# Turning two heads, two key tiles and two output tiles per block of transposes, and moving the context states beside the first level products

## The chip, the cores and the metric

The kernel runs as one program on one core of a Trainium2 chip. The metric is device time in microseconds, the median of several runs. TensorE (PE) multiplies and transposes and writes to PSUM, eight banks of 128 x 512 words in float32; ScalarE (ACT) and VectorE (DVE) read PSUM and work in SBUF; SyncE (SP) and GpSimd (POOL) issue most transfers. Each engine takes its instructions from a queue in a fixed order and waits for semaphores of the others.

## The reference

One block of a network with two branches on 256 tokens of width 2048, with 256 context tokens beside them:

```python
xn = rmsnorm(h, norm_gain) * (1 + scale) + shift        # cn for the context likewise
aq, ak, av, ag, hq, hff, hfb, hi, hg, ma, mb = split_columns(xn @ w_in)
# branch 1: window attention, 16 heads in 4 groups, keys of tokens and of context, one sink logit per head
att_branch = window_attention(q, k, v, k_c, v_c, sink) * silu(ag)
# branch 2: a gated linear recurrence in both directions; the context gives its start states
s_f = hgrn2_final_state(ck_f, cv_h, cg_f)               # s_b from the flipped context
o = hgrn2_bidir(q_h, v_h, k_f, g_f, k_b, g_b, s_f, s_b)
hg_branch = rmsnorm_per_head(o) * silu(hg)
y = sigmoid(ma + b0) * (hg_branch @ w_o_hgrn) + sigmoid(mb + b1) * (att_branch @ w_o_attn)
out = rmsnorm(h + gate * (y @ w_out)) * final_gain
```

## The kernel before

Nearly all time goes into products with weights in float32. Each weight chunk (128 x 1024 values) is loaded, rounded by ACT into `wh` (line 76), and DVE takes the rest `wl = raw - wh` (line 77); a product is then three float32r matmuls of 512 columns, high by high, low by high, high by low (`mm3`, lines 82 to 85). Three buffers each of `wh` and `wl` and four of `raw` go round. One chunk feeds 12 to 24 matmuls. Results `pj` rotate through four PSUM banks. The other four banks have one buffer each and are called `tp`, `o`, `al1` and `al2`.

Between these projections stands work in plain float32: transposes (a matmul against the identity) and small products. A function that does such work is a generator; each `yield` hands over to a generator of projection chunks, the filler, so that PE has weights to multiply while ACT and DVE prepare the next step. In the recurrence `weave` (line 739) takes as many filler chunks as the yielded number says, in units of 24 matmuls of 512 columns. In the attention `alternate` (line 751) takes a fixed number of chunks per yield.

Inside `tc.manual_schedule(engines={PE})` the order on PE is the order in which the program is written. ACT, DVE, SP and POOL are ordered at build time by a planner, which simulates the machine and at each moment gives an engine the ready instruction of highest priority: attention has 2 * PRIO, weight chunks PRIO, the rest none. The resulting order is fixed in each queue. From line 1045 on PE too is left to the planner.

The steps around the change:

- `pair` (line 476), eight times, two heads of the recurrence each. Lines 623 to 625 turn the outputs of the pair before (`to`, four transposes into `tp`). Lines 627 to 633 transpose the four decay blocks `E` into `tw` and copy them as `wT` into the second half of the tile `X2`. After a unit of filler, lines 635 to 645 multiply `wT` with the context values into `sb` (16 products of 128 columns, bank `o`), the context states, which ACT copies negated. Then `grow` (VectorE) and `copies` (ScalarE) prepare the level products; `grow(1)` writes its totals `TT` into the second half of `X2`, where `wT` lies. After 1.5 units, 128 products in column strips of 32 (`level`, line 562, bank `a1`) follow.
- `keys` (line 927): four key tiles, four transposes each into `tp`, each followed by a `split`: ACT copies the bank rounded (line 884), DVE subtracts that from the bank (line 885). Two filler chunks after each tile.
- `attend` (line 971): 35 iterations. Iteration n computes the scores of head n (`scores`, three matmuls into `al1` or `al2` by turns, then mask, maximum, exponential, scaling by DVE and ACT into `pr`), one filler chunk, then for every fourth head the product with the values (`values`, 12 matmuls into `o`, evicted by line 1011 and split into `bH`, `bL`), then `turned(n - 2)`: the probabilities of head n - 2 are transposed into `tp` and split into `pT`; then one more filler chunk. A score product starts only when the last readers of its bank are done.
- `part_b` (line 1053): for each of four column blocks the merged output `y` of the two token tiles, by two DVE operations each (lines 1057 and 1058), is transposed into `tp` and split.

Of the kernel before, what the change touches and what calls it, by code (L numbers as in the profile page):

```python
# [7 lines left out]
F32 = mybir.dt.float32  # L8
F32R = mybir.dt.float32r
U8 = mybir.dt.uint8  # L10
AF = mybir.ActivationFunctionType
# [3 lines left out]
P = 128  # L15
# [23 lines left out]
def block_kernel(ctx: ExitStack, tc: tile.TileContext, x, c, cx, c_ctx, w_ada, b_ada, norm_gain, w_in,  # L39
# [14 lines left out]
    ps = ctx.enter_context(pl("ps", 1, space=PSUM))  # L54
# [119 lines left out]
    def alt():  # L174
        turn[0] ^= 1
        return f"al{turn[0] + 1}"
# [299 lines left out]
    def pair(g, p, grp, F, banks_q):  # L476
# [52 lines left out]
        def copies(b):  # L529
            for slots, a in ((kslot, 0), (qslot, 1)):  # L530
                if b in slots:
                    dst, src = slots[b], mix(a, 3 - 2 * a, 0, 512, b)
                    if len(dst.shape) == 3:
                        for h in range(2):
                            act.activation(dst[:, h].rearrange("p (n two b) -> p n two b", two=2, b=b),
                                           mix(a, 3 - 2 * a, h * T, T, b), AF.Copy)
                    else:
                        act.activation(dst.rearrange("p (n two b) -> p n two b", two=2, b=b), src, AF.Copy)  # L538
# [49 lines left out]
        def grow(b):  # L588

            n2 = 512 // (2 * b)  # L590
            if b == 1:
                even = [F[d][:, :, 0:T].rearrange("p h (n two) -> p h n two", two=2)[:, :, :, 0] for d in range(2)]
                odd = [F[d][:, :, 0:T].rearrange("p h (n two) -> p h n two", two=2)[:, :, :, 1] for d in range(2)]
            else:
                tv = tots[b].rearrange("p d (n two) -> p d n two", two=2)
                even, odd = tv[:, :, :, 0], tv[:, :, :, 1]
            toff = 1024 - 2 * 512 // b
            Tn = TT[:, toff: toff + 2 * n2].rearrange("p (d n) -> p d n", d=2)
            if b == 1:
                for d in range(2):  # L600
                    for a, par, f in ((d, 0, odd[d]), (2 + d, 1, even[d])):
                        av = v3(A[:, a, :]).rearrange("p h (n two) -> p h n two", two=2)[:, :, :, par]
                        dve.tensor_tensor(av, av, f, op=ALU.mult)
                    dve.tensor_tensor(v3(Tn[:, d, :]), even[d], odd[d], op=ALU.mult)
            else:
                for a0, par, f in ((0, 0, odd), (2, 1, even)):
                    av = A[:, a0: a0 + 2, :].rearrange("p a (n two b) -> p a n two b", two=2, b=b)[:, :, :, par, :]
                    dve.tensor_tensor(av, av, f.unsqueeze(3).to_broadcast([P, 2, n2, b]), op=ALU.mult)  # L608
                dve.tensor_tensor(Tn, even, odd, op=ALU.mult)
            tots[2 * b] = Tn  # L610
# [7 lines left out]
            return ps.tile([P, 512], F32, tag=alt(), name="al")  # L618

        copies(1)  # L620
        yield 0.5

        for f in done:
            f()
        done[:] = []
        yield 0.5
        wT = X2[:, 1024:].rearrange("p (a s) -> p a s", a=8)
        for d in range(2):
            tw = ps.tile([P, 512], F32, tag=alt(), name="tw")
            for i in range(2):  # L630
                for s in range(2):
                    pe.transpose(tw[:, (2 * i + s) * P: (2 * i + s + 1) * P], E[:, d, i, s * P: (s + 1) * P], ident)
            act.activation(wT[:, 4 * d: 4 * d + 4, :], tw.rearrange("p (a b) -> p a b", a=4), AF.Copy)
        yield 1.0
        so = hp.tile([P, 2, 512], F32, tag="so", name="so")
        qslot[64] = so[:, 1]
        S = so[:, 0, :].rearrange("p (d h v) -> p d h v", d=2, h=2)
# [1 line left out]
        for d in range(2):  # L639
            for i in range(2):  # L640
                o = sb[:, (2 * d + i) * HD: (2 * d + i + 1) * HD]
                for s in range(2):
                    pe.matmul(o, wT[:, 4 * d + 2 * i + s, :], vc[:, s, (2 * p + i) * HD: (2 * p + i + 1) * HD],  # L643
                              start=s == 0, stop=s == 1)
        act.activation(so[:, 0, :], sb, AF.Copy, scale=-1.0)

        grow(1)
        copies(2)
        grow(2)
        copies(4)  # L650
        yield 1.5
        a1 = al_bank()
        for z, b in enumerate((0, 1, 2, 4)):
            level(a1, z * P, b)
        for b in (4, 8, 16, 32):
            grow(b)
            copies(2 * b)
# [225 lines left out]
    def split(dh, dl, src, **kw):  # L883
        act.activation(dh, src, AF.Copy, **kw)
        dve.tensor_tensor(dl, src, dh.bitcast(F32), op=ALU.subtract)
# [11 lines left out]
    with tc.manual_schedule(engines={mybir.EngineType.PE}):  # L897
# [27 lines left out]
            split(XH[:, rows, :], XL[:, rows, :], bv[t].rearrange("p (r c) -> p r c", r=2))  # L925

        def keys():
            for t in range(4):
                tk = ps.tile([P, 512], F32, tag="tp", name="tkk")
                for j in range(4):  # L930
                    pe.transpose(tk[:, j * P: (j + 1) * P], kr[:, t, j, :], ident)

                dst = [X[:, t // 2: 8: 2, (t % 2) * P: (t % 2 + 1) * P] for X in (XH, XL)]
                split(dst[0], dst[1], tk.rearrange("p (j t) -> p j t", j=4))
                yield

        def group_in(j, st):
# [33 lines left out]
        def attend(sts):  # L971

            prs, pTs = {}, {}

            def scores(n):
                j, t, i = n // 8, n // 4 % 2, n % 4
                h = 4 * j + i
                sc = ps.tile([P, 512], F32, tag=alt(), name="sc")
                mm3(sc.rearrange("p (a k) -> p a k", a=2), [X[:, t, i, :] for X in sts[j]["q"]], k_mov(j), True, True)
                mt = sc[:, (1 - t) * P: (2 - t) * P]  # L980
                tri = cs[:, K_TRI + t * P: K_TRI + (t + 1) * P]
                mx = few.tile([P, 4], F32, tag="mx", name="mx", bufs=4)
                dve.tensor_tensor(mt, mt, tri, op=ALU.add)
                dve.tensor_reduce(mx[:, 0:1], sc, mybir.AxisListType.X, ALU.max)
                dve.tensor_scalar(mx[:, 1:2], mx[:, 0:1], sk[:, h: h + 1], -1.0, op0=ALU.max, op1=ALU.mult)
                pr = base.tile([P, 512], F32, tag="sm", name="pr", bufs=3)
                act.activation(pr, sc, AF.Exp, bias=mx[:, 1:2], accum_out=mx[:, 2:3])
                act.activation(mx[:, 3:4], sk[:, h: h + 1], AF.Exp, bias=mx[:, 1:2])
                dve.tensor_tensor(mx[:, 2:3], mx[:, 2:3], mx[:, 3:4], op=ALU.add)
                dve.reciprocal(mx[:, 2:3], mx[:, 2:3])  # L990
                act.activation(pr, pr, AF.Copy, scale=mx[:, 2:3])
                prs[n] = pr

            def turned(n):
                i = n % 4
                if i == 0:
                    pTs[n // 4] = [at.tile([P, 4, 4, P], F32R, tag=tg, name="pT") for tg in ("A", "X2")]
                pT = pTs[n // 4]
                tk = ps.tile([P, 4, P], F32, tag="tp", name="tkp")
                for q in range(4):  # L1000
                    pe.transpose(tk[:, q, :], prs[n][:, q * P: (q + 1) * P], ident)  # L1001
                split(pT[0][:, :, i, :], pT[1][:, :, i, :], tk)

            def values(m):
                j, t = m // 2, m % 2
                pT = pTs[m]
                ob = ps.tile([P, 512], F32, tag="o", name="oba")
                for kt in range(4):
                    mm3(ob, v_st(kt, j), [X[:, kt].rearrange("p h t -> p (h t)") for X in pT], kt == 0, kt == 3)
                br = base.tile([P, 4, P], F32, tag="bb", name="br", bufs=2)  # L1010
                dve.tensor_tensor(br, ob.rearrange("p (h t) -> p h t", h=4), sts[j]["g"][:, :, t * P: (t + 1) * P],
                                  op=ALU.mult)
                hs = slice(4 * j, 4 * j + 4)
                split(bH[:, hs, t * P: (t + 1) * P], bL[:, hs, t * P: (t + 1) * P], br)

            for n in range(35):
                if n < 32:
                    with tc.high_priority(2 * PRIO):
                        scores(n)
                yield  # L1020
                with tc.high_priority(2 * PRIO):
                    if n % 4 == 2 and n > 2:
                        values(n // 4 - 1)
                    if 2 <= n < 34:
                        turned(n - 2)
                yield

# [10 lines left out]
            yield from gates_b(1)  # L1038

        sts = [{} for _ in range(4)]  # L1040
        alternate(keys(), group_in(0, sts[0]), 2)
        alternate(attend(sts), fill(sts), 1)


# [8 lines left out]
    def part_b(n):  # L1053
        by = proj_tok(w_oa, n * 512, b_st, range(2))
        for t in range(2):
            yt = base.tile([P, 512], F32, tag="sm", name="yt", bufs=3)
            dve.tensor_tensor(yt, by[t], sgb[n][:, t, :], op=ALU.mult)  # L1057
            dve.tensor_tensor(y[n][:, t, :], y[n][:, t, :], yt, op=ALU.add)
            tk = ps.tile([P, 4, P], F32, tag="tp", name="tky")
            for i in range(4):  # L1060
                pe.transpose(tk[:, i, :], y[n][:, t, i * P: (i + 1) * P], ident)
            ks = slice(4 * n, 4 * n + 4)
            split(XH[:, ks, t * P: (t + 1) * P], XL[:, ks, t * P: (t + 1) * P], tk)

    for n in range(4):
        part_b(n)
# [126 lines left out]
```

## Time and profile before

| | us |
|---|---|
| median of 3 runs (lowest, highest) | 1636.56 (1636.43, 1636.96) |
| the profiled execution's own time | 1636.14 |
| its span, first to last instruction | 1634.3 |
| PE busy | 1613.9 (99%) |
| DVE busy | 937.0 (57%) |
| ACT busy | 763.4 (47%) |
| recurrence, 190 to 900 us: PE busy | 710.0 of 710 |
| attention, 1160 to 1412 us: PE busy; DVE; ACT | 251.5; 179.5; 180.4 of 252 |

The granted TensorE clock was 0.997 over the span. Times within the trace count from the first instruction. In a timeline row the first number is the start, the second the duration, and `x4` says that four alike instructions were merged into the row; what stands in brackets is the idle time of the engine before it and what ended it. The end of a matmul is modelled, so the distance from start to start is the better measure on PE.

### The profile page before, as it was taken

What the parts mean: (1) busy time and instruction counts of PE and PEld (TensorE: products, weight loads), DVE (VectorE), ACT (ScalarE), POOL (GpSimd) and SP (SyncE); (2) the same over time, 40 slices, a digit from 0 to 9 for tenths busy, and PEclk for the clock granted to TensorE, in tenths of its full rate; (3) what the DMA queues carried; (4) which work ended last, traced back from release to release, by engine and by line L of the source; (5) the groups of instructions that cost most, each with busy time, mean ns of one, the idle gap of its engine ahead of it and who ended that gap; (6) DMA issues with size and microseconds to landing.
All of it is one profiled execution on the core that took longest, in us unless ns stands there. A gap on an engine that the chain in (4) does not pass through costs nothing.

```text
span 1634.3 us, 24809 instructions
## 1 busy us (share of the span) xinstructions
PE 1613.9 (99%) x9882; PEld 1329.3 (81%) x9882; DVE 937.0 (57%) x1463; ACT 763.4 (47%) x1200; POOL 31.4 (2%) x88
## 2 busy tenths in 40 slices
PE   7999999999999999999999999999999999999998
PEld 4558888888888888888888888888888888788887
DVE  4444467536665466645567455235677676555565
ACT  4333454424553345433566443224576787454443
POOL 2000000000000000000000000000000000000000
PEclk9999999999999999999999999999999999999999
DMA  9993444336343453435335555424544454665554
GB/s 356 383 384 109 142 150 149 110 127 195 104 129 117 156 176 106 131 117 177 118 119 176 186 193 193 129 90 142 179 140 146 133 168 157 231 201 192 184 191 140
DMA packets 191427, 274.89 MB, mean 168 GB/s; under 512 B 9776, under 2 KB 112592, under 8 KB 190544
## 3 DMA queue, kind: packets, MB, share of 16 engines
q1 hardware_dynamic: 189344, 268.95, 50.1%
q0 software_dynamic: 1248, 3.25, 0.7%
q8 instruction: 77, 1.26, 0.3%
q10 hardware_dynamic: 720, 1.11, 0.2%
q14 instruction: 38, 0.31, 0.1%
HBM read 271.17 MB, written 2.11 MB: 167 GB/s over the span
## 4 chain that ended last, share of the span: by engine, by line
PE 95%; DMA 2%; DVE 1%; issue 1%; ACT 0%; SPq 0%; POOLq 0%; POOL 0%; ACTq 0%
PE pj L83 24%; PE pj L85 23%; PE pj L84 23%; PE pj L141 7%; PE pj L146 4%; DMA raw<-in_w_ada_dram 2%; PE pa L306 2%; PE al L562 1%; PE pj L396 1%; PE pj L389 1%; PE sb L643 1%; PE tkp L1001 1%; PE pj L390 1%; PE oba L83 0%; PE sc L85 0%
## 5 line engine op out<-in xcount | busy, mean ns | idle before, releaser
L77 DVE TENSOR_TENSOR wl<-raw,wh 128x1024 fp32r<-128x1024 f32 x392 | 479.6, 1224 | 425.4 <-ACT wh L76 425.0
L76 ACT ACTIVATE wh<-raw 128x1024 fp32r<-128x1024 f32 x392 | 414.7, 1058 | 589.4 <-PE pj L85 428.6
L84 PE MATMUL pj<-wl,xHL 128*128 128x512 f32 (+1 forms) x1024 | 395.6, 386 | 0.4 <-DVE wl L77 0.4
L85 PE MATMUL pj<-wh,xHL 128*128 128x512 f32 (+1 forms) x1024 | 395.4, 386 | 0.0
L83 PE MATMUL pj<-wh,xHL 128*128 128x512 f32 (+1 forms) x1024 | 391.4, 390 | 0.0
L85 PEld LDWEIGHTS pj<-wh,xHL 128*128 128x128 f32 x1024 | 192.4, 188 | 39.0
L84 PEld LDWEIGHTS pj<-wl,xHL 128*128 128x128 f32 x1024 | 192.5, 188 | 38.2 <-DVE wl L77 0.7
L83 PEld LDWEIGHTS pj<-wh,xHL 128*128 128x128 f32 x1024 | 192.2, 188 | 37.8 <-DVE yt L1057 0.4
L141 PE MATMUL pj<-xHL,wh 128*128 128x512 f32 x512 | 181.1, 396 | 0.0
L83 PE MATMUL pj<-xHL,wh 128*128 128x512 f32 x416 | 164.6, 396 | 0.0
L85 PE MATMUL pj<-xHL,wl 128*128 128x512 f32 x416 | 162.1, 390 | 0.0
L84 PE MATMUL pj<-xHL,wh 128*128 128x512 f32 x416 | 162.0, 389 | 0.0
L146 PE MATMUL pj<-xHL,wl 128*128 128x256 f32 x512 | 139.9, 283 | 0.0
L141 PEld LDWEIGHTS pj<-xHL,wh 128*128 128x128 f32 x512 | 95.0, 188 | 19.2
L84 PE MATMUL pj<-wl,bH 128*128 128x512 f32 x256 | 99.9, 390 | 0.0
L85 PE MATMUL pj<-wh,bL 128*128 128x512 f32 x256 | 99.6, 389 | 0.0
L146 PEld LDWEIGHTS pj<-xHL,wl 128*128 128x128 f32 x512 | 96.7, 189 | 2.5
L85 PEld LDWEIGHTS pj<-xHL,wl 128*128 128x128 f32 x416 | 78.1, 188 | 16.7
L83 PEld LDWEIGHTS pj<-xHL,wh 128*128 128x128 f32 x416 | 78.1, 188 | 15.5
L84 PEld LDWEIGHTS pj<-xHL,wh 128*128 128x128 f32 x416 | 78.2, 188 | 15.4
L83 PE MATMUL pj<-wh,bH 128*128 128x512 f32 x256 | 89.8, 390 | 0.1
L608 DVE TENSOR_TENSOR A<-A,X 128x512 f32<-128x512 f32 x96 | 62.0, 687 | 16.7 <-ACT qk L538 6.7
(278 smaller groups left out, 1688.2 us busy)
## 6 DMA issues: line engine op xcount, KB each, us to landing
raw<-in_w_in_dram SPq DMA_DIRECT2D x292, 512.0 KB, 3.5
raw<-in_w_ada_dram SPq DMA_DIRECT2D x128, 256.0 KB, 5.5
raw<-in_w_ada_dram SPq DMA_DIRECT2D x32, 512.0 KB, 3.7
raw<-in_w_o_hgrn_dram SPq DMA_DIRECT2D x32, 512.0 KB, 3.5
raw<-in_w_o_attn_dram SPq DMA_DIRECT2D x32, 512.0 KB, 3.7
raw<-in_w_out_dram SPq DMA_DIRECT2D x32, 512.0 KB, 4.3
raw<-in_w_in_dram SPq DMA_DIRECT2D x24, 256.0 KB, 5.5
X<-in_x_dram SPq DMA_DIRECT2D x2, 1024.0 KB, 6.7
```

Source lines behind the costliest of these rows:

```text
L76: act.activation(h[:, :n], raw[:, :n], AF.Copy)
L77: dve.tensor_tensor(lo[:, :n], raw[:, :n], h[:, :n].bitcast(F32), op=ALU.subtract)
L83: pe.matmul(o, s[0], m[0], start=first, stop=False)
L84: pe.matmul(o, s[0], m[1], start=False, stop=False)
L85: pe.matmul(o, s[1], m[0], start=False, stop=last)
L141: pe.matmul(banks[i].rearrange("p (a t) -> p a t", a=2), h[:, j, cs_], xHL[:, :, kt, :T], start=kt == 0, stop=kt == KT - 1)
L146: pe.matmul(banks[i][:, :T], lo[:, j, cs_], xH[:, kt, :T], start=False, stop=False)
L306: pe.matmul(pa[32 * g: 32 * g + 32, : 2 * w], cT[:, k0 + g, :], rv_[:, :, g % nk, :], start=k0 == 0, stop=k0 == KT - 4, tile_position=(0, ...
L389: pe.matmul(o, hw, xH[:, kt, :], start=kt == 0, stop=False)
L390: pe.matmul(o, lo[:, kt - k, cs_], xH[:, kt, :], start=False, stop=False)
L396: pe.matmul(o, hw, xL[:, kt, :], start=False, stop=kt == KT - 1)
L608: dve.tensor_tensor(av, av, f.unsqueeze(3).to_broadcast([P, 2, n2, b]), op=ALU.mult)
```

## The change

Five edits, all in the order and the placing of the work; the arithmetic is the same.

1. `pair`: the two yields of 0.5 around the turning of the previous outputs become one of 1.0 ahead of it, so that `to` and `tw` are written one behind the other. `wT` now overwrites `E` in the first half of `X2`. `grow(1)`, `copies(2)`, `grow(2)`, `copies(4)` come directly behind that, then one yield of 2.5, then the 16 context products, and directly behind them the level products. The negated copy of the states follows the level products in the program.
2. `keys`: two tiles' transposes in a row, into `tp` and `o`, then both splits; four filler chunks after each pair of tiles.
3. `scores`: the bank is `al1` for even heads and `al2` for odd ones.
4. `turned`: called on even iterations only; it transposes heads n - 2 and n - 1 in a row, the first into `tp`, the second into `al2`, then splits both.
5. `part_b`: both tiles' merges first, then eight transposes into `tp` and `o` inside a region that orders PE's instructions among themselves, then both splits.

```diff
@@ pair
         copies(1)
-        yield 0.5
+        yield 1.0
         for f in done:
             f()
         done[:] = []
-        yield 0.5
-        wT = X2[:, 1024:].rearrange("p (a s) -> p a s", a=8)
+        wT = X2[:, :1024].rearrange("p (a s) -> p a s", a=8)
...
-        yield 1.0
+        grow(1)
+        copies(2)
+        grow(2)
+        copies(4)
+        yield 2.5
...
-        act.activation(so[:, 0, :], sb, AF.Copy, scale=-1.0)
-        grow(1)
-        copies(2)
-        grow(2)
-        copies(4)
-        yield 1.5
         a1 = al_bank()
         for z, b in enumerate((0, 1, 2, 4)):
             level(a1, z * P, b)
+        act.activation(so[:, 0, :], sb, AF.Copy, scale=-1.0)
@@ keys
-            for t in range(4):
-                tk = ps.tile([P, 512], F32, tag="tp", name="tkk")
...
+            for z in range(2):
+                tks = [ps.tile([P, 512], F32, tag=tg, name="tkk") for tg in ("tp", "o")]
+                for t in range(2):
+                    for j in range(4):
+                        pe.transpose(tks[t][:, j * P: (j + 1) * P], kr[:, 2 * z + t, j, :], ident)
...
@@ attend
-                sc = ps.tile([P, 512], F32, tag=alt(), name="sc")
+                sc = ps.tile([P, 512], F32, tag=f"al{n % 2 + 1}", name="sc")
...
-                tk = ps.tile([P, 4, P], F32, tag="tp", name="tkp")
-                for q in range(4):
-                    pe.transpose(tk[:, q, :], prs[n][:, q * P: (q + 1) * P], ident)
-                split(pT[0][:, :, i, :], pT[1][:, :, i, :], tk)
+                tks = [ps.tile([P, 4, P], F32, tag=tg, name="tkp") for tg in ("tp", "al2")]
+                for i in range(2):
+                    for q in range(4):
+                        pe.transpose(tks[i][:, q, :], prs[n + i][:, q * P: (q + 1) * P], ident)
+                for i in range(2):
+                    z = (n + i) % 4
+                    split(pT[0][:, :, z, :], pT[1][:, :, z, :], tks[i])
...
-                    if 2 <= n < 34:
+                    if n % 2 == 0 and 2 <= n < 34:
                         turned(n - 2)
...
-        alternate(keys(), group_in(0, sts[0]), 2)
+        alternate(keys(), group_in(0, sts[0]), 4)
@@ part_b
-            tk = ps.tile([P, 4, P], F32, tag="tp", name="tky")
-            for i in range(4):
-                pe.transpose(tk[:, i, :], y[n][:, t, i * P: (i + 1) * P], ident)
+        tks = [ps.tile([P, 4, P], F32, tag=tg, name="tky") for tg in ("tp", "o")]
+        with tc.manual_schedule(engines={mybir.EngineType.PE}):
+            for t in range(2):
+                for i in range(4):
+                    pe.transpose(tks[t][:, i, :], y[n][:, t, i * P: (i + 1) * P], ident)
+        for t in range(2):
             ks = slice(4 * n, 4 * n + 4)
-            split(XH[:, ks, t * P: (t + 1) * P], XL[:, ks, t * P: (t + 1) * P], tk)
+            split(XH[:, ks, t * P: (t + 1) * P], XL[:, ks, t * P: (t + 1) * P], tks[t])
```

More of the change, by code (lines that the diff above doesn't have):

```diff
@@ L927, in keys @@
         def keys():
-            for t in range(4):
-                tk = ps.tile([P, 512], F32, tag="tp", name="tkk")
[L930 to L934, printed above, removed]
+            for z in range(2):
[4 more added lines that the diff above has]
+                for t in range(2):
+                    dst = [X[:, z: 8: 2, t * P: (t + 1) * P] for X in (XH, XL)]
+                    split(dst[0], dst[1], tks[t].rearrange("p (j t) -> p j t", j=4))
                 yield
@@ L994, in turned @@
             def turned(n):
-                i = n % 4
-                if i == 0:
+                if n % 4 == 0:
                     pTs[n // 4] = [at.tile([P, 4, 4, P], F32R, tag=tg, name="pT") for tg in ("A", "X2")]
                 pT = pTs[n // 4]
-                tk = ps.tile([P, 4, P], F32, tag="tp", name="tkp")
-                for q in range(4):
-                    pe.transpose(tk[:, q, :], prs[n][:, q * P: (q + 1) * P], ident)
-                split(pT[0][:, :, i, :], pT[1][:, :, i, :], tk)
+                tks = [ps.tile([P, 4, P], F32, tag=tg, name="tkp") for tg in ("tp", "al2")]
[5 more added lines that the diff above has]
+                    split(pT[0][:, :, z, :], pT[1][:, :, z, :], tks[i])
             def values(m):
@@ L1058, in part_b @@
             dve.tensor_tensor(y[n][:, t, :], y[n][:, t, :], yt, op=ALU.add)
-            tk = ps.tile([P, 4, P], F32, tag="tp", name="tky")
-            for i in range(4):
-                pe.transpose(tk[:, i, :], y[n][:, t, i * P: (i + 1) * P], ident)
+        tks = [ps.tile([P, 4, P], F32, tag=tg, name="tky") for tg in ("tp", "o")]
[3 more added lines that the diff above has]
+                    pe.transpose(tks[t][:, i, :], y[n][:, t, i * P: (i + 1) * P], ident)
+        for t in range(2):
             ks = slice(4 * n, 4 * n + 4)
-            split(XH[:, ks, t * P: (t + 1) * P], XL[:, ks, t * P: (t + 1) * P], tk)
+            split(XH[:, ks, t * P: (t + 1) * P], XL[:, ks, t * P: (t + 1) * P], tks[t])
     for n in range(4):
```

## The prediction

> **What bounds the kernel now.** I read the profile's page first, then PE's waits, then PE's timeline at the places that the change touches, and last ACT and DVE between a turning and the score product behind it. Busy time and the chain of work:
>
> ```profile
> span 1634.3 us, 24809 instructions
> ...
> PE 1613.9 (99%) x9882; PEld 1329.3 (81%) x9882; DVE 937.0 (57%) x1463; ACT 763.4 (47%) x1200; POOL 31.4 (2%) x88
> ...
> PE 95%; DMA 2%; DVE 1%; issue 1%; ACT 0%; SPq 0%; POOLq 0%; POOL 0%; ACTq 0%
> ```
>
> PE bounds the kernel: every instruction that PE no longer issues or no longer waits for shortens the end, and every wait put into its queue lengthens it. In the attention and the recurrence PE's waits hold only one group:
>
> ```profile
> PE oba L83 <- DVE qTa L950: 0.5, 3, 0.2
> ```
>
> So no transposed bank and no score bank makes PE wait today. The change takes away no wait that stands in its way; it can gain only what PE loses at the seams between float32r products and float32 transposes.
>
> **What a seam costs.** PE's timeline, first around eight transposes in a row (`tw`), then around four (`tkp`):
>
> ```profile
> 193.84 0.39 PE L85 MATMUL pj<-wh,xHL 128*128 128x512 f32 x1
> ...
> 197.24 0.39 PE L85 MATMUL pj<-wh,xHL 128*128 128x512 f32 x1
> 197.47 1.03 PE L632 MATMUL tw<-cs,X 128*128 128x128 f32 x8
> ...
> 198.57 0.39 PE L84 MATMUL pj<-wl,xHL 128*128 128x512 f32 x1
> ...
> 203.81 1.95 PE L643 MATMUL sb<-vc,X 128*128 128x128 f32 x16
> ...
> 213.54 0.39 PE L85 MATMUL pj<-wh,xHL 128*128 128x512 f32 x1
> 213.86 0.46 PE L562 MATMUL al<-qk 128*32 128x32 f32 x32
> ```
>
> ```profile
> 1179.21 0.60 PE L1001 MATMUL tkp<-cs,pr 128*128 128x128 f32 x4
> ...
> 1179.89 0.39 PE L84 MATMUL pj<-wl,xHL 128*128 128x512 f32 x1
> ...
> 1182.42 0.39 PE L83 MATMUL sc<-xHL,qTa 128*128 128x512 f32 x1
> ```
>
> Fifteen undisturbed products lie between 193.84 and 197.24: 3.40 / 15 = 0.227 us each. From the first of four transposes to the second product behind them are 1179.89 - 1179.21 = 0.68, of which one product is 0.23: four transposes cost 0.45. Eight cost 198.57 - 197.47 - 0.23 = 0.87. Two blocks of four cost 0.03 more than one of eight. The products behind a block are slightly slow: 11 between 1179.89 and 1182.42, 0.230 each, make 11 x 0.0033 = 0.036 per block; 23 between 198.57 and 203.81, 0.228 each, make about 0.026. If that tail too is paid once, a merge saves 0.03 + 2 x 0.036 - 0.026 = 0.08. Bounds 0.03 and 0.08; I take 0.05, since the tail's cause isn't in the rows.
>
> **The change part by part.** The number of transposes, products, splits and DMAs is the same.
>
> Merges: `turned` goes from 32 blocks to 16, `keys` from 4 to 2, `part_b` from 8 to at best 4, and `to` joins `tw` in the last pair (in the other pairs the two already follow each other). That is 16 + 2 + 4 + 1 = 23 merges of 0.05: **-1.1 us** (19 of 0.03 to 23 of 0.08: -0.6 to -1.8).
>
> The context states: 16 products leave a place between float32r products and stand ahead of the strips of `level`. The entry into the strips costs 213.86 - 213.54 = 0.32 instead of 0.23, so 0.09 per pair. If that vanished behind `sb`, eight pairs would give -0.7. But strips behind a block of full-width transposes pay it too:
>
> ```profile
> 27.23 1.04 PE L410 MATMUL idle<-cs 128*128 128x128 f32 x8
> 28.20 1.06 PE L306 MATMUL pa<-raw,cT 128*32 128x512 f32 x8
> ```
>
> Eight transposes are 0.87 and the strips start after 0.97, so 0.10 remain. I take **0** (-0.7 to +0.1, eight times 0.01). The Trainium skill ("TensorEngine Tiling (Array Packing)", Key Properties) says that a change of tiling mode drains TensorE; by that rule the seam merely moves from products to states and the gain is 0, while the -0.7 would need a free change; both entries in the rows agree with it.
>
> `grow(1)` now writes beside `wT` instead of over it, so DVE no longer waits there for the states; DVE sets nothing in this stage (PE is busy throughout), so 0. One copy of the states (like other 512-column copies, 0.6 on ACT) moves into the stretch ahead of the second levels. There the last `grow` ends well before `kt` reads it:
>
> ```profile
> 228.71 1.29 DVE L608 TENSOR_TENSOR A<-A,X 128x512 f32<-128x512 f32 x2
> ...
> 235.80 0.66 PE L669 MATMUL kt<-cs,A 128*128 128x128 f32 x4
> ```
>
> That is 5.8 us of cover; the copy and what it pushes back cost 0, and 0.6 per pair if the cover were gone.
>
> Two heads' probabilities are read earlier: an odd head is turned one iteration sooner. The tightest is head 7, scaled at 1220.10 and turned with head 6 from 1223.39 on:
>
> ```profile
> 1220.10 0.71 ACT L991 ACTIVATE pr<-pr,mx 128x512 f32<-128x512 f32 x1
> ...
> 1223.39 0.60 PE L1001 MATMUL tkp<-cs,pr 128*128 128x128 f32 x4
> ```
>
> 2.6 us remain, so no wait. Each `values` gets its last head two chunks earlier, no wait either.
>
> **The new wait.** The second head goes through `al2`, and the next score product (odd heads) writes `al2`. It must wait until ACT and then DVE have split that bank, and everything behind it on PE waits too. Iteration 12, with the work that lies between:
>
> ```profile
> 1252.61 0.60 PE L1001 MATMUL tkp<-cs,pr 128*128 128x128 f32 x4
> 1252.81 1.06 ACT L76 ACTIVATE wh<-raw 128x1024 fp32r<-128x1024 f32 x1 [2.43 <-PE pj L141]
> ...
> 1253.77 0.58 ACT L884 ACTIVATE pT<-tkp 128x512 fp32r<-128x512 f32 x1
> 1254.08 1.22 DVE L77 TENSOR_TENSOR wl<-raw,wh 128x1024 fp32r<-128x1024 f32 x1
> ...
> 1255.34 0.69 DVE L885 TENSOR_TENSOR pT<-tkp,pT 128x512 fp32r<-128x512 f32 x1
> ...
> 1255.84 0.40 PE L83 MATMUL sc<-xHL,qTa 128*128 128x512 f32 x1
> ```
>
> A chunk ends just ahead of the turning, which frees a weight buffer; so `wh` is ready before the transposed bank and goes first on ACT, and `wl` goes first on DVE. The split ends at 1256.03, after the score product has started; today nobody minds, because `tp` isn't needed for two more chunks. Iteration 14, where `values` evictions share the queues:
>
> ```profile
> 1272.79 0.64 ACT L884 ACTIVATE bH<-br 128x512 fp32r<-128x512 f32 x1
> 1272.83 0.69 DVE L885 TENSOR_TENSOR pT<-tkp,pT 128x512 fp32r<-128x512 f32 x1
> 1273.36 0.40 PE L83 MATMUL sc<-xHL,qTa 128*128 128x512 f32 x1
> 1273.45 0.69 DVE L885 TENSOR_TENSOR bL<-br,bH 128x512 fp32r<-128x512 f32 x1
> ```
>
> The first split in iterations 2, 8 and 10 (iteration 2's next score product is the row of 1182.42 above):
>
> ```profile
> 1182.15 0.69 DVE L885 TENSOR_TENSOR pT<-tkp,pT 128x512 fp32r<-128x512 f32 x1
> ...
> 1226.49 0.69 DVE L885 TENSOR_TENSOR pT<-tkp,pT 128x512 fp32r<-128x512 f32 x1
> 1226.60 0.39 PE L83 MATMUL sc<-xHL,qTa 128*128 128x512 f32 x1
> ...
> 1239.32 0.60 PE L1001 MATMUL tkp<-cs,pr 128*128 128x128 f32 x4
> ...
> 1240.59 0.69 DVE L885 TENSOR_TENSOR pT<-tkp,pT 128x512 fp32r<-128x512 f32 x1
> ...
> 1242.53 0.39 PE L83 MATMUL sc<-xHL,qTa 128*128 128x512 f32 x1
> ```
>
> And what a wait of this kind costs PE beyond its length, from the one that exists:
>
> ```profile
> 1206.38 0.69 DVE L950 SCALAR_TENSOR_TENSOR qTa<-tkq,qTa 128x512 fp32r<-128x512 f32 x1
> 1206.57 0.40 PE L141 MATMUL pj<-xHL,wh 128*128 128x512 f32 x1
> 1207.12 0.50 PE L83 MATMUL oba<-pT,xHL 128*128 128x512 f32 x1 [0.15 <-DVE qTa L950]
> 1207.46 0.40 PE L84 MATMUL oba<-pT,xHL 128*128 128x512 f32 x1
> ```
>
> DVE ends at 1207.07, the product starts 0.05 later, and the next comes 0.34 after it instead of 0.23: 0.16 on top. Back-to-back DVE operations of 512 columns start 1273.45 - 1272.83 = 0.62 apart, so the second split ends 0.62 + 0.69 = 1.31 after the first one starts; the score product would start 0.44 later than now (four more transposes ahead of it). Lateness plus 0.16:
> - iterations like 12 (4, 12, 20): 1255.34 + 1.31 = 1256.65 against 1256.28, so 0.37 + 0.16 = 0.53;
> - like 14 (6, 14, 22): 1274.14 against 1273.80, 0.50 directly behind the first split, 1.12 with `bL` between (0.62 more);
> - like 8 (8, 16, 24): 1227.80 against 1227.04, 0.92;
> - iteration 2: 1183.46 against 1182.86, 0.76;
> - like 10 (10, 18, 26): 1241.90 against 1242.97, no wait; the last ones lie near zero and are left out.
>
> Sum 3 x 0.53 + 3 x 0.92 + 0.76 = 5.1, plus 3 x 0.50 to 3 x 1.12: 6.6 to 8.5, middle 7.5. Against that, odd iterations now have no split, which takes 0.6 each out of ACT's and DVE's queues ahead of the next turning. I give back 0.5 at iterations like 8, where ACT's queue is full, 0.2 at those like 12: 2.1. **+5.4 us.**
>
> The existing wait of `oba` costs 1207.12 - 1206.57 - 0.23 + 0.11 = 0.43, three times 1.3; with a split less ahead of it DVE comes sooner; I take **-0.4** (0 to -1.3).
>
> Sum: 1636.14 (own time of the profiled execution, span 1634.3 and 1.8 around it) - 1.1 - 0.4 + 5.4 = 1640.0. The median is 0.42 above that execution, so **1640.5 us**.
>
> **The rivals.**
> - *The second split is in time.* If ACT takes both banks ahead of `wh`, the second split can end about 2.6 after the first transpose (iteration 10: 1241.90 - 1239.32), and the score product comes after 1182.42 - 1179.21 + 0.44 = 3.65. It decides in favour from the point where the first DVE split starts within 2.3 of the first transpose. For it: priority 2 * PRIO; against it: `wh` is ready first in three of four kinds of turning. Then the merges alone remain, not slower: 1636.56 - 1.1 - 0.4 = 1635.1.
> - *The wait is larger:* nothing is given back and `bL` comes between: 8.5 - 0.6 = 7.9, so 1644.5.
> - *`part_b` doesn't merge.* The region only orders PE's instructions among themselves; the planner may still put a product between the two tiles' transposes. Four merges of 0.05 are lost: 1640.7, inside the forecast.
> - *Merges save more than the rows show,* over 0.2 per seam: 23 x 0.2 - 5.4 is still no gain, so this needs the first rival too: 1632.
>
> **How the numbers follow.** Forecast with a wait of some size, 1637.5 to 1643.5: 0.62; split in time: 0.30; larger wait: 0.05; larger saving: 0.03. A difference under 0.2% (3.3 us) can't be told from none. Of the forecast's case 0.37 of its 0.62 lie above 1639.8, with the larger wait slower is 0.42; of the second case 0.02 falls below 1633.3, so faster is 0.05; same 0.53. The range leaves out half of each outer case: 1634.6 to 1644.0.
>
> **What would show it.** A group of PE's waits "sc L83 <- DVE pT", some 10 times and up to 1 us each; attention longer by 3 to 5 us, the rest within 1; eight-fold `tkp` rows; levels still entered with 0.1 of delay. It is wrong if no score product waits, if odd heads' `tkp` waits for `pr`, or if the recurrence changes by over 1 us.

## The result and the profile after

The changed kernel takes **1651.78 us**, median of 5 runs (1650.43 to 1652.84); the kernel before took 1636.75 beside it (1636.43 to 1637.27). The ratio is 1.0090, with 95% between 1.0079 and 1.0101: slower by 15 us. The profiled execution of the changed kernel is the longest of its five, 1652.84 with a span of 1651.0, 16.7 us above the profiled span of before. The page of the changed kernel, span, busy time and shares of the chain of work:

```profile
span 1651.0 us, 24818 instructions
...
PE 1617.9 (98%) x9882; PEld 1332.6 (81%) x9882; DVE 936.9 (57%) x1463; ACT 765.4 (46%) x1200; POOL 31.4 (2%) x88
...
PE 91%; ACT 4%; DVE 2%; DMA 1%; issue 1%; POOLq 0%; POOL 0%; ACTq 0%; DVEq 0%
```

PE issues the same 9882 matmuls and is still on the chain for nearly all of it, but ACT, which had 0% of the chain, now has 4%: PE waits for it. Busy time of DVE and ACT is what it was, so nobody does more work. The groups of PE's waits in the attention (releaser, total, count, median):

```profile
PE sc L83 <- DVE pT L884: 10.9, 8, 2.1
...
PE oba L83 <- DVE qTa L951: 2.3, 3, 0.8
```

The first group is new; the second was 0.5 for its three. The score products of both kernels (count, durations, start of the first to start of the last), before and then after:

```profile
L83 PE MATMUL sc<-xHL,qTa x32: 389/389/398, 1163.6 to 1391.9; 128*128 128x512 f32 x32
```

```profile
L83 PE MATMUL sc<-xHL,qTa x32: 389/392/501, 1164.7 to 1410.6; 128*128 128x512 f32 x32
```

The stretch from the first to the last score product grew from 228.3 to 245.9, by 17.6. That is all of the loss: the other stages together differ by -0.9 (start +1.15, recurrence +0.2, keys -0.25, `part_b` -0.1, the handover from the attention to the outputs -1.9).

Inside the 17.6, I took PE's distances from start to start and counted what exceeds 0.227. In front of the first score product behind a turning PE stands for these times, by iteration: 2: 0.63; 4, 12, 20: 0.12, 0.20, 0.20; 6, 14, 22: 1.01, 1.01, 1.05; 8, 16, 24: 2.21, 2.26, 2.18; 28: 1.82; the others 0. Sum **12.7**. The product behind each of them comes late as well, 1.2 in all. `oba` takes 1.8 more. Four transposes more lie in the window, 0.4. The last 1.6 stand in one place: behind the wait of iteration 8 the next nine products start 0.33 to 0.43 apart instead of 0.227. The TensorE clock that was granted there was half (stretch, its length, PE's busy time and matmuls, granted clock, DMA share, GB/s):

```profile
1234.20:1236.70 2.50, 2.50 (x7) 0.50 0.36 106
```

No other wait of the attention is followed by such a stretch in this trace. These five make 17.7, which is all of it to within 0.1.

Iteration 8 shows the largest wait (start, duration, engine, line, operation; in brackets the idle time before it and what ended it):

```profile
1227.30 1.03 PE L1003 MATMUL tkp<-cs,pr 128*128 128x128 f32 x8
1227.74 1.04 ACT L76 ACTIVATE wh<-raw 128x1024 fp32r<-128x1024 f32 x1
...
1229.00 0.58 ACT L883 ACTIVATE pT<-tkp 128x512 fp32r<-128x512 f32 x1
1229.60 1.28 ACT L988 ACT_TABLE_LOAD   x1
1230.30 0.68 DVE L884 TENSOR_TENSOR pT<-tkp,pT 128x512 fp32r<-128x512 f32 x1
1230.89 0.69 ACT L988 ACTIVATE pr<-sc,mx 128x512 f32<-128x512 f32 x1
1231.76 0.58 ACT L883 ACTIVATE pT<-tkp 128x512 fp32r<-128x512 f32 x1
1232.37 0.69 DVE L884 TENSOR_TENSOR pT<-tkp,pT 128x512 fp32r<-128x512 f32 x1 [0.33 <-ACT pT L883]
...
1233.11 0.50 PE L83 MATMUL sc<-xHL,qTa 128*128 128x512 f32 x1 [2.05 <-DVE pT L884]
```

Read ACT's rows downward. `wh` goes first, then, behind an activation of a gate that is not shown, the copy of the first bank at 1229.00. The copy of the second bank could follow at 1229.6; but ACT first loads its table (1.28) and takes the exponential of the current head (0.69), and comes to the second bank only at 1231.76. DVE is idle meanwhile but for one small operation and subtracts at 1232.37, and PE, which holds the next score product at the head of its queue, starts it 0.05 after DVE ends.

Iteration 6, where `values` has just been evicted:

```profile
1214.86 0.57 ACT L883 ACTIVATE pT<-tkp 128x512 fp32r<-128x512 f32 x1
1215.43 0.63 ACT L883 ACTIVATE bH<-br 128x512 fp32r<-128x512 f32 x1
...
1215.96 0.58 ACT L883 ACTIVATE pT<-tkp 128x512 fp32r<-128x512 f32 x1
1216.09 0.69 DVE L884 TENSOR_TENSOR bL<-br,bH 128x512 fp32r<-128x512 f32 x1
1216.70 0.68 DVE L884 TENSOR_TENSOR pT<-tkp,pT 128x512 fp32r<-128x512 f32 x1
...
1217.44 0.50 PE L83 MATMUL sc<-xHL,qTa 128*128 128x512 f32 x1 [0.84 <-DVE pT L884]
```

`bH` stands between the two copies, `bL` between the two subtractions. Iterations 12 and 28:

```profile
1260.31 1.03 PE L1003 MATMUL tkp<-cs,pr 128*128 128x128 f32 x8
...
1261.47 1.07 ACT L883 ACTIVATE pT<-tkp 128x512 fp32r<-128x512 f32 x2
...
1262.87 1.28 DVE L884 TENSOR_TENSOR pT<-tkp,pT 128x512 fp32r<-128x512 f32 x2
...
1264.20 0.50 PE L83 MATMUL sc<-xHL,qTa 128*128 128x512 f32 x1
```

```profile
1389.08 1.04 PE L1003 MATMUL tkp<-cs,pr 128*128 128x128 f32 x8
...
1390.36 1.28 ACT L988 ACT_TABLE_LOAD   x1
...
1392.52 1.07 ACT L883 ACTIVATE pT<-tkp 128x512 fp32r<-128x512 f32 x2
...
1394.54 0.50 PE L83 MATMUL sc<-xHL,qTa 128*128 128x512 f32 x1 [1.66 <-DVE pT L884]
```

In iteration 12 both copies follow each other, and so do both subtractions: the wait is 0.20. In iteration 28 both copies follow each other too, but behind a table load and an exponential.

### The profile page after: what moved, and what is told of

Same layout as the page of the kernel before. It is cut to its first block, busy times and chain, and to the rows that moved or that the text cites. A ratio compares the mean times of both kernels' runs of the same rounds, so it can differ in the third digit from the quotient of the medians.

```text
span 1651.0 us, 24818 instructions
## 1 busy us (share of the span) xinstructions
PE 1617.9 (98%) x9882; PEld 1332.6 (81%) x9882; DVE 936.9 (57%) x1463; ACT 765.4 (46%) x1200; POOL 31.4 (2%) x88
## 4 chain that ended last, share of the span: by engine, by line
PE 91%; ACT 4%; DVE 2%; DMA 1%; issue 1%; POOLq 0%; POOL 0%; ACTq 0%; DVEq 0%
PE pj L83 23%; PE pj L85 23%; PE pj L84 23%; PE pj L141 6%; PE pj L146 3%; PE pa L306 2%; PE al L562 1%; PE pj L396 1%; PE pj L389 1%; PE sb L648 1%; PE pj L390 1%; DMA raw<-in_w_ada_dram 1%; ACT wh L76 1%; ACT L969 1%; ACT L988 1%
```

## The experiments

The theory after the result was the predicted one in a larger size: the next score product needs `al2`, and `al2` is free only when the second head is split. The rivals: turning two heads at once loads ACT and DVE in bursts, so that PE waits somewhere whatever bank is used; or the other edits have a share in it.

**One head per turning again.** The attention is put back, the edits of `pair`, `keys` and `part_b` stay.

```diff
-                sc = ps.tile([P, 512], F32, tag=f"al{n % 2 + 1}", name="sc")
+                sc = ps.tile([P, 512], F32, tag=alt(), name="sc")
...
-                tks = [ps.tile([P, 4, P], F32, tag=tg, name="tkp") for tg in ("tp", "al2")]
...
+                tk = ps.tile([P, 4, P], F32, tag="tp", name="tkp")
...
-                    if n % 2 == 0 and 2 <= n < 34:
+                    if 2 <= n < 34:
```

> The changed kernel with only the attention's turning put back: one head per turning into tp, score banks by turns as before; the pair, key and output edits stay. Theory A (the whole loss is PE's waiting in the attention for splits that the turning of two heads makes late: 12.7 us at the score products, 1.3 behind them, 1.8 more at oba): the time returns to 1636.75 less the few merges that are left, 1636.0 to 1636.6. Rival B (the other edits, or the planner's new order that they bring, carry a part of the loss): over 1638.

Measured: 1636.37 against 1636.53, ratio 0.9999 (0.9990 to 1.0009). The three other edits together change nothing that can be measured, and the loss belongs to the attention.

**The second head in another bank.** First `o`, which queries and `values` use:

```diff
-                tks = [ps.tile([P, 4, P], F32, tag=tg, name="tkp") for tg in ("tp", "al2")]
+                tks = [ps.tile([P, 4, P], F32, tag=tg, name="tkp") for tg in ("tp", "o")]
```

> The changed kernel with the second head's transposes in bank o in place of al2. Theory A: the score products no longer wait; the next users of o (the query transposes tkq, twice per group of four iterations pairs, and the value products) wait instead, less often: 1637.5 to 1643. Rival C (two heads in one go overload ACT and DVE in even iterations, so weight chunks or evictions come late whatever the bank is): 1648 or more, with the waits at pj.

Measured: 1651.11, ratio 1.0084 (1.0067 to 1.0101). The time lies where rival C put it, but not for its reason: no `pj` waits. The waits of the score products are gone, and as much stands in another place, which the expectation of theory A had far too small. PE's waits, and one of them in the timeline:

```profile
PE tkp L1003 <- ACT pT L883: 6.5, 3, 2.2
PE tkp L1003 <- DVE br L1015: 4.1, 4, 1.1
```

```profile
1210.51 0.60 PE L1003 MATMUL tkp<-cs,pr 128*128 128x128 f32 x4
...
1213.26 1.08 PE L1003 MATMUL tkp<-cs,pr 128*128 128x128 f32 x4 [2.15 <-ACT pT L883]
```

The wait sits in the middle of the block: four transposes go, and the other four wait until bank `o`, which `values` has just filled, is evicted. For three of the seven waits the profile names the first head's copy, which ends at 1213.15 here; the eviction (DVE, line 1015) ends at 1213.11, and the transposes start 0.15 after that, as they do where the profile names the eviction (1245.34 after 1245.19). So the wait isn't a matter of the bank `al2` as such: it is inherited by whoever needs a bank that is still being read.

Next, one of the four banks through which the projections rotate:

```diff
-                tks = [ps.tile([P, 4, P], F32, tag=tg, name="tkp") for tg in ("tp", "al2")]
+                tks = [ps.tile([P, 4, P], F32, tag="tp", name="tkp"),
+                       pj.tile([P, 4, P], F32, tag="pj", name="tkp")]
```

> The changed kernel with the second head's transposes in one of the four rotating pj banks. Theory A: no score product waits; what is left is the wait of oba for the query split (2.3 us by the trace after): 1637 to 1640, with at most 2 us of new waits of a projection for its bank. Rival C: 1648 or more.

Measured: 1636.61 against 1636.53, ratio 1.0000 (0.9991 to 1.0010), 0.4 below theory A's range. Two heads are still turned in one go and still split one behind the other, and the 15 us are gone. That fells the rival that bursts cost by themselves. Only one group of waits is left in the attention, that of `oba`, and at 2.3 for its three it is as large as in the changed kernel. One of them in the timeline:

```profile
1205.77 0.71 ACT L992 ACTIVATE pr<-pr,mx 128x512 f32<-128x512 f32 x1
1206.38 0.58 ACT L950 ACTIVATE qTa<-tkq 128x512 fp32r<-128x512 f32 x1
1206.99 0.69 DVE L951 SCALAR_TENSOR_TENSOR qTa<-tkq,qTa 128x512 fp32r<-128x512 f32 x1 [0.55 <-ACT qTa L950]
...
1207.73 0.50 PE L83 MATMUL oba<-pT,xHL 128*128 128x512 f32 x1 [0.76 <-DVE qTa L951]
```

In the kernel before, ACT took the queries at once:

```profile
1205.76 0.58 ACT L949 ACTIVATE qTa<-tkq 128x512 fp32r<-128x512 f32 x1
```

An odd head's probabilities are now read one iteration sooner, and the order on ACT has their scaling ahead of the queries' copy; that the planner puts it there for this reason was not tested. `oba` writes the bank `o`, in which the transposed queries `tkq` stand, and so waits 0.76 instead of 0.15.

**The banks exchanged.** The first head goes into `al2`, the second into `tp`.

```diff
-                tks = [ps.tile([P, 4, P], F32, tag=tg, name="tkp") for tg in ("tp", "al2")]
+                tks = [ps.tile([P, 4, P], F32, tag=tg, name="tkp") for tg in ("al2", "tp")]
```

> The changed kernel with the two banks of a turning exchanged: the first head into al2, the second into tp. Work, order of the transposes and of the splits are the same; only the score product now waits for the first split, not for the second. By the first splits' ends in the trace after (1216.15 against a due 1216.43, 1230.98 against 1230.90, 1282.22 against 1282.49) Theory A gives waits of under 2 us in all at the score products: 1638 to 1641. Rival C: 1648 or more.

Measured: 1638.28, ratio 1.0011 (1.0002 to 1.0021). The one wait of a score product that is left, beside the 2.3 of `oba`:

```profile
PE sc L83 <- DVE pT L884: 1.0, 1, 1.0
```

The work, its amount and the four banks are those of the changed kernel, and 13.5 of 15.2 us are gone. The score product waits for the split of the head that stands in its own bank. When that is the first split, it is in time to within 0.15 in all turnings but iteration 28.

**What stands between the two copies.** The second head's rounding goes from ACT to DVE, out of the queue with the table load; `al2` stays.

```diff
-                    split(pT[0][:, :, z, :], pT[1][:, :, z, :], tks[i])
+                    dh, dl = pT[0][:, :, z, :], pT[1][:, :, z, :]
+                    if i:
+                        dve.tensor_copy(dh, tks[i])
+                        dve.tensor_tensor(dl, tks[i], dh.bitcast(F32), op=ALU.subtract)
+                    else:
+                        split(dh, dl, tks[i])
```

> The changed kernel (second head in al2) with the rounding of the second head by DVE in place of ACT: the same number of operations, but no ACT work between the transposed bank and its release. Theory A2 (most of the wait beyond the forecast is ACT's queue: the exponential with its table load, or bH, stands between the two copies): the waits at the score products fall from 10.9 us to under 4: 1638 to 1643. Rival E (DVE's own queue makes the second split late): 1646 or more.

Measured: 1644.81, ratio 1.0049 (1.0035 to 1.0063). That is in neither range: the waits fall from 10.9 to 4.7 + 1.5 = 6.2, not to under 4. PE's waits at the score products, and iteration 8:

```profile
PE sc L83 <- DVE pT L1009: 4.7, 6, 1.4
...
PE sc L83 <- DVE mx L990: 1.5, 3, 0.5
```

```profile
1226.39 1.04 PE L1003 MATMUL tkp<-cs,pr 128*128 128x128 f32 x8
1227.52 0.68 DVE L1008 CAST pT<-tkp 128x512 fp32r<-128x512 f32 x1
...
1229.58 0.68 DVE L1009 TENSOR_TENSOR pT<-tkp,pT 128x512 fp32r<-128x512 f32 x1
1230.41 0.47 PE L83 MATMUL sc<-xHL,qTa 128*128 128x512 f32 x1 [0.25 <-DVE pT L1009]
```

In the iterations like 8 the wait falls from 2.2 to 0.4: there it was indeed ACT's queue, with the table load and the exponential. In iterations 2 and 28 it goes as well, from 0.6 and 1.8 to 0 and 0.1. In those like 14 it rises from 1.0 to 1.5, and in those like 12 from 0.2 to 0.67 (the second group: there the profile names a small DVE operation right behind the second split), since DVE's queue now holds one operation more. So the cause is the order of the queue that the second split goes through; ACT's was the worse one in iterations like 8, in 2 and in 28, DVE's in those like 12 and 14.

**The queries in `tp`.** On top of the version with the `pj` bank, the transposed queries leave bank `o`, so that `oba` no longer waits for them; the same edit is then made alone in the kernel before.

```diff
-                tk = ps.tile([P, 512], F32, tag="o", name="tkq")
+                tk = ps.tile([P, 512], F32, tag="tp", name="tkq")
```

> The kernel with the second head in a pj bank, and the query transposes tkq in bank tp in place of o, so that the value products no longer wait for the query split. Theory A: the three waits of oba (2.3 us, with restart 2.8 against 1.0 before) go, and the merges (16 at 0.02 to 0.055 by the rows, 2 keys, 4 outputs) come out at last: 1633.0 to 1635.0. Rival D (the waits only move to tp, whose first split then holds up tkq or the next turning): 1636 to 1639.

> The kernel before with only the query transposes moved from o to tp. Its three waits of oba cost 0.43 each by the rows. Theory A: 1635.2 to 1635.8. Rival D: 1636.5 or more. The distance to the run with merges then tells what the merges save by themselves: 0.6 to 1.8 by the prediction.

Measured: with two heads per turning 1633.55 against 1636.60, ratio 0.9981 (0.9972 to 0.9989), and no wait of PE is left between 130 and 1600 us; alone in the kernel before 1637.45, ratio 1.0004 (0.9995 to 1.0013). There the wait has moved, to the next turning in `tp`, and grown from 0.5 to 1.7, as rival D has it (waits of that run):

```profile
PE tkp L1001 <- DVE qTa L950: 1.7, 3, 0.6
```

**Is it the merges or the banks?** The version with the queries in `tp` merges 23 times and also has one more bank for turned heads. First the `pair` edit is taken out of it:

```diff
-        yield 1.0
+        yield 0.5
         for f in done:
             f()
         done[:] = []
+        yield 0.5
...
-        grow(1)
-        copies(2)
-        grow(2)
-        copies(4)
-        yield 2.5
+        yield 1.0
...
+        act.activation(so[:, 0, :], sb, AF.Copy, scale=-1.0)
+        grow(1)
+        copies(2)
+        grow(2)
+        copies(4)
+        yield 1.5
```

> The run with second head in pj and queries in tp, with the pair edit undone: context states again one unit and a half ahead of the level products, two yields of 0.5. By the blocks on PE states and levels cost 3.23 us per pair apart (1.80 + 1.43) and 3.22 to 3.25 together. Theory A: no difference beyond 0.3 us to the run with the pair edit. Rival F (a change of tiling mode saved, 0.09 per pair): 0.7 us slower than it.

Measured: 1633.19, ratio 0.9979 (0.9970 to 0.9988), 0.4 less than with it, which the intervals don't tell from none. Moving the context states is worth nothing that can be measured.

Then the kernel before, with the queries in `tp` and the heads turned one by one, no merge anywhere, by turns in `tp` and in a `pj` bank. Odd heads in `tp`:

```diff
-                tk = ps.tile([P, 4, P], F32, tag="tp", name="tkp")
+                if i % 2:
+                    tk = ps.tile([P, 4, P], F32, tag="tp", name="tkp")
+                else:
+                    tk = pj.tile([P, 4, P], F32, tag="pj", name="tkp")
```

> The kernel before, one head per turning, with query transposes in tp and the heads' transposes by turns in pj and tp, so that neither oba nor a turning waits for the query split. No merge anywhere. By the rows the waits of oba cost 1.37 in all: Theory A, that merges save about 0.02 per seam and that the two-head turning gains 1.4 more at the handover to the output products (PE waited there for bH, for a bank and for wl before), expects 1635.0 to 1635.6, 1.5 to 2 over the run with two heads in tp and pj. Rival G (the 3 us of that run are the banks' alone): 1633.5 to 1634.2.

Measured: 1636.21, ratio 0.9998 (0.9989 to 1.0007). That is beyond both ranges, because the run does not do what its expectation supposes: the three waits stand where they stood, 1.7 in all.

The heads turned right behind the queries are 3, 11 and 19, all odd; they went into `tp`, as the queries did. With the test the other way round (`if i % 2 == 0`), they go into `pj`:

> As the run before, one head per turning and no merge, with the two banks exchanged: even heads in tp, odd heads in pj. In the run before three turnings of odd heads (3, 11 and 19) waited 1.7 us in tp for the query split, 2.2 with restart; they are now in pj. Theory A: no wait is left in the attention, and the time is 1636.2 - 2.2 = 1634.0 (1633.6 to 1634.5); what the run with two heads per turning has beyond it (1633.55 and 1633.19 by two runs) is all that the merges are worth, 0.4 to 0.9. Rival H (merges are worth 2 us or more): over 1635.2.

Measured: 1633.57 against 1636.27, ratio 0.9983 (0.9974 to 0.9992). A kernel that merges nothing is, within the intervals, as fast as the ones that merge (0.9981 and 0.9979). It gains 2.7 over the kernel before beside it, they 3.1 and 3.4; what is left for the merges is under 1 us and can't be told from none. So at least 2.7 come from which bank the turned heads and the queries stand in. All three beat both kernels of this case.

## Why the prediction was wrong

The forecast was 1640.5 in a range up to 1644.0; the time is 1651.78. The mechanism is the predicted one, with its group of waits, its engine and its line. Its size was 13.9 us (12.7 and the late products behind) where the prediction has 5.4; in the profiled execution the half clock behind one of the waits adds 1.6 that the prediction has no term for.

- **PE bounds the kernel: right.** The attention is 17.6 longer by waits in PE's queue and what they bring with them, and the kernel 16.7.
- **The seams, -1.1: right in sign, too large.** A block of eight transposes in the attention of the changed kernel:

```profile
1247.09 1.04 PE L1003 MATMUL tkp<-cs,pr 128*128 128x128 f32 x8
1248.20 0.40 PE L84 MATMUL pj<-wl,xHL 128*128 128x512 f32 x1
...
1250.70 0.39 PE L83 MATMUL sc<-xHL,qTa 128*128 128x512 f32 x1
```

  1248.20 - 1247.09 - 0.23 = 0.88 where the prediction has 0.87, and the 11 products behind take 2.50 / 11 = 0.227 each. But over the whole attention, from the first to the last score product, measured as the 228.3 above, the version with the queries in `tp` takes 227.09 with 14 merges, 226.64 without the four transposes by which its window holds more; the unmerged one takes 226.96. That is 0.32 / 14 = 0.02 per merge, below the lower bound of 0.03. At 23 merges it is some 0.5 us, which no time here can show.
- **The context states, 0: right.** The place of the strips in the changed kernel:

```profile
213.11 1.95 PE L648 MATMUL sb<-vc,X 128*128 128x128 f32 x16
214.98 0.46 PE L562 MATMUL al<-qk 128*32 128x32 f32 x32
...
216.55 0.39 PE L84 MATMUL pj<-wl,xHL 128*128 128x512 f32 x1
```

  States and strips together take 216.55 - 213.11 - 0.23 = 3.21; apart they took 1.80 and 1.43, together 3.23. The entry into the strips is paid behind full-width products of either kind. The Trainium skill ("TensorEngine Tiling (Array Packing)", Key Properties) says that a change of tiling mode drains TensorE, and moving the states leaves as many changes as before. The trace agrees: 3.21 against 3.23.
- **Probabilities in time, recurrence unchanged: right.** No turning waits for `pr`; PE is busy for 710.0 of 710 us in the recurrence, as before.
- **The new wait: the step that failed is "the second split ends 0.62 + 0.69 = 1.31 after the first one starts".** It puts the two splits directly behind each other. In iteration 8 the first starts at 1230.30 on DVE and the second ends at 1233.06, 2.76 later; in iteration 6 it is 1.92, with `bL` between. The trace of before had the sign of it, on ACT, where the prediction shows only DVE for iteration 8:

```profile
1225.19 0.58 ACT L884 ACTIVATE pT<-tkp 128x512 fp32r<-128x512 f32 x1
1225.79 1.28 ACT L987 ACT_TABLE_LOAD   x1
...
1227.95 1.05 ACT L76 ACTIVATE wh<-raw 128x1024 fp32r<-128x1024 f32 x1
```

  The table load, and behind it the exponential, follow directly on the copy in iterations 8, 16, 24 and 28 of the kernel before, and in no other. A second copy that has to come behind them starts at 1227.95 and its DVE half, as in the trace after, 0.61 later; with 0.69 for that half it ends at 1229.25 against a due 1227.04. This estimate from rows of before gives a wait of 2.2, which is what came. The kinds, the prediction's numbers (which hold 0.16 for the late product) beside the measured wait alone:

| iterations | predicted, each | measured, each | what lay between |
|---|---|---|---|
| 8, 16, 24 | 0.92 | 2.2 | table load and exponential between ACT's two copies |
| 6, 14, 22 | 0.50 to 1.12 | 1.0 | `bH` and `bL`, the upper bound |
| 4, 12, 20 | 0.53 | 0.2 | nothing; DVE came sooner (by 0.17 in iteration 12) |
| 2 | 0.76 | 0.6 | nothing |
| 28 | "near zero", left out | 1.8 | table load and exponential ahead of both copies |

  In the sum that is 6.65 for the iterations like 8 where the prediction has 2.8, and 1.8 for iteration 28 where it has nothing. The 2.1 "given back" came only in the iterations like 12. In those like 8, from which 1.5 of it was taken, nothing came back. The run with the rounding on DVE shows that ACT's queue makes the 2.2; it doesn't show why the build-time planner chose that order, though `turned` and the softmax have the same priority.
- **`oba`, -0.4: wrong in sign.** It is +1.8 (three times 0.76 instead of 0.15; the product behind is as late as before, 0.11). The step that failed is "with a split less ahead of it DVE comes sooner". The split was gone, but the scaling of the odd head took a place ahead of the queries' copy on ACT, and DVE can only follow ACT.
- **The rivals.** The split in time didn't come: it is what iteration 10 shows, but in 11 of 15 turnings the split was late. The larger wait was nearest, with 7.9 too small as well: it gives nothing back and lets `bL` come between, but not the table load. `part_b` did merge: its transposes in the changed kernel come in four blocks of eight (from 1448.0, 1492.4, 1536.9 and 1559.5 on), and the run with one head per turning shows that they are worth nothing measurable.
- **The range.** Its upper end lets one operation, `bL`, come between the two splits. With the table load and the exponential of the order of before between them too, by the estimate above, three iterations have 2.4 in place of 0.92 and iteration 28 has 1.8 (both with the late product): some 14.5 us in place of 8.5, near the 13.9 that came. And the order of before is itself a result of the planner: any operation that is ready on ACT at that moment (table load and exponential, 1.97) can come between, so a bound that lets only the old neighbours in is none.

## What to carry to other kernels

Before an operation is put into a PSUM bank, ask which instruction of PE writes that bank next, and whether it stands at the head of PE's queue before both readers are done: the same eight transposes cost 15 us in `al2`, nothing in a rotating `pj` bank, and under 2 us when two banks were merely exchanged. When a queue is ordered anew by a planner, price a wait with what stands directly behind the first operation on each queue in the old order, and with the longest operation that is ready there, not by the mere length of the operations themselves. And measure whether a gain comes from the merge or from the bank that came with it: here an unmerged kernel with one more bank had 2.7 of the 3.1 to 3.4 us.

## What the runs showed that was not expected

Joining two blocks of transposes saves some 0.02 us on PE, so that even 23 of them can't be seen.

A wait goes over to whoever uses the bank next: from the score product (`al2`) to the middle of the block of transposes (`o`), and from `oba` to the turning (queries in `tp`).

The granted clock can fall behind a wait of some 2 us, and need not. In the changed kernel it was 0.50 for about 3 us behind the wait of 2.05 in iteration 8, which cost 1.6 more, and 1.00 behind those of 2.10 and 2.02 in iterations 16 and 24; with the second head in `o` it fell to 0.50 behind two of the three waits of 2.15 to 2.20 in the middle of a block. What decides it is not in these rows.

PE also loses 1.6 us in the kernel before at the handover from the attention to the outputs, which the prediction didn't look at. Waits of the weight loads there, between 1391 and 1440 us:

```profile
PEld pj L84 <- DVE wl L77: 0.7, 1, 0.7
PEld pj L83 <- ACT bH L884: 0.5, 1, 0.5
PEld pj L83 <- DVE yt L1057: 0.4, 1, 0.4
```

All three stand, as large, in the two other versions that turn heads in `tp` alone, and none of them in the changed kernel or in those with `pj` as a second bank, merged or not. Nor do they stand in the other versions with a second bank (`o`, or the two exchanged). So they go with the second bank for the turned heads; by which step it clears them was not followed. It fits the version with the `pj` bank, which ends level with the kernel before: it gains these 1.6 and loses 1.8 at `oba`.
